# Weight sums moved into the first down stage, projection weights split without a rounded copy, and another place for small states, in a streaming encoder step

## The chip, the cores and the metric

One core of one Trainium2 chip runs the whole program. Its engines are TensorE (PE in the profile, PEld its weight loads), VectorE (DVE), ScalarE (ACT), GpSimd (POOL) and SyncE (SP), which here issues nearly all DMAs from one queue. The metric is the device time of one execution in microseconds, and the median of the runs counts. All numbers are float32; products are made from high and low parts of float32 operands.

## The reference, cut to what matters

The reference is one layer over 1024 prompt tokens and 64 sample tokens of width 1024:

```
h = x + 0.5 * (silu(n(x) @ Wg) * (n(x) @ Wu)) @ Wd      # first FFN, inner width 2816
z = n(h) @ w_in            -> u | q | k | v
y_ssm = GLU(S5(u)); y_att = DiffAttn(q, k, v)
h = h + concat(y_ssm, y_att) @ w_out
h = h + CrossAttn(n(h), n(mem))
x = h + 0.5 * (second FFN)(n(h));  final RMSNorm
```

The outputs are the normed tokens, the new keys and values, the last S5 states and the memory's keys and values. `w_out` and the rows of `Wd` are inputs, so everything that depends on them alone can be computed at any time before it is used.

## The kernel before, in words

**The products.** Activations lie feature by token, 128 features by 1088 tokens (a "row" of the pool `rows`, which has 36 of them). Each float32 product is three matmuls, from high and low parts of weight and operand (`mm3`, line 176 in the profile). Large products are made in Winograd's form: seven products of half-sized blocks in place of eight, with sums of weight quarters and sums of activation quarters. The sums of gate/up weights are made on POOL beside the products (`mixed`, lines 672 to 675). The sums of down weights are made on POOL by `down_sums` (lines 502 to 510) and stored in DRAM (`down_d`), those of the square products (`w_out`, `w_cq`, `w_co`) by `weight_sums` (lines 442 to 450, `sums_d`); both load weight quarters on SP, do four additions on POOL (lines 506 to 509 and 446 to 449) and store.

**The split.** A weight tile of 128x512 is split by `split_into` (lines 152 to 154): ACT writes the rounded high part `hi` to SBUF and a second rounded copy `q` to the one buffer of a PSUM pool `pr`; DVE subtracts `q` from the raw tile. With `staged=False` `w_split` (lines 162 and 163) leaves the copy out, and DVE subtracts `hi`, which lies in SBUF. `units` (line 183), which makes the 16 input projections and the 4 GLU products, uses the staged form; the memory projections use the other.

**The first FFN.** `ffn` first makes gate and up for 22 blocks j of the inner width. After the first five blocks `aside(j)` takes one step of the generator `side` after each product, seven in a block. The side of the first FFN is a chain: `s5_params` (S5 coefficients, small DVE operations, then transposes on PE in line 1086), `diff_lambda`, `s5_prep` for four groups, and `down_sums` for all blocks of the down product, with the four rows `prep` as its places and two steps for a piece. Of what is left when the blocks are done, `for _ in side: pass` issues the rest. Then the down product runs in three blocks b (`DOWN`: 4, 8 and 8 rows of Wd), each in seven factors q of four products i. Each product is emptied by `residual` (line 783, DVE) or, for four factors of the first block, by ACT; `prepare` makes the next factor's weight split (lines 152 to 154) and operand (`value`, line 412; `operand`, lines 418 and 419), and `fetch` loads the weights of the third next factor. In the last block `join` (line 834) adds accumulators on POOL and DVE. Two last rows of Wd are done per output row: `residual`, then `mix_row`, which splits the row (lines 212 and 213), adds its square to the statistics (`Stats.add`, lines 259 and 260, POOL) and stores it.

**The stage after it.** `wide_powers` makes S5 powers on POOL in `wide_row`. Then come 16 input projections (`in_unit`); after each half of one, every generator in `bg` is taken a step: `weight_sums(0)` of `w_out` from the first unit on, four `s5_main` (the scans on DVE, products in lines 1344 and 1345, gelu on ACT in line 1346), and from the third head on `weight_sums` of `w_co` and `w_cq`. `s5_main` keeps small states `gs` (128x152, lines 1307 to 1325) in a buffer of the tag `ws`, of which there are four and in which `weight_sums` also has its quarters.

**What sets the order.** Of each engine and queue the instructions run in order. The order is planned when the program is built: instructions are taken by their place in the code as soon as a simulated timeline has their inputs and buffers free. A wait that lasts longer on the chip than in the plan holds all that is behind it on its engine.

## Time and profile before

| | us |
|---|---|
| median of 3 runs | 2386.49 |
| lowest and highest | 2383.15, 2392.55 |
| the profiled execution | 2393.03 |
| its span, first to last instruction | 2391.2 |
| mean granted TensorE clock | 0.980 |

In the profile PE is TensorE, DVE VectorE, ACT ScalarE, POOL GpSimd, SPq SP's DMA queue. L176 is line 176 of the kernel. `r<-b,r` is a tile written and the tiles read (b is a PSUM bank, r a row, wr, ws, wh and wl weight tiles). A clock of 1.00 is 2.4 GHz, 0.50 is 1.2 GHz. "Idle before it" is the time for which the engine had nothing to run, with what ended it.

### The profile page before, as it was taken

Reading aid. Unit: us, or ns where it says so; the run is one execution under the profiler, and the core shown is the slowest. Engines: PE = TensorE matmul, PEld = TensorE weight load, DVE = VectorE, ACT = ScalarE, POOL = GpSimd, SP = SyncE. Lnnn points to the kernel's source line nnn. Section 1 sums busy time; section 2 is a strip of 40 time slices with the busy share of each in tenths; the row PEclk is TensorE's granted clock in tenths of the full one; section 3 lists DMA queues with packets and bytes.
Section 4 is the critical chain, followed back from the end, with each engine's and each line's share of the span. In section 5 each row is a group of like instructions: output and inputs, shape, how many; then the busy total and the mean of one; then the engine's idle time right before and its main releaser. Section 6 shows DMA issues by size and latency. Waiting matters only on the chain.

```text
span 2391.2 us, 45853 instructions
## 1 busy us (share of the span) xinstructions
PE 2265.2 (95%) x16914; PEld 2202.8 (92%) x16914; DVE 1599.6 (67%) x3318; ACT 1289.3 (54%) x2506; POOL 1083.4 (45%) x1048
## 2 busy tenths in 40 slices
PE   6999999998999898998999999898999999999998
PEld 6999999998999897997789999798899999999998
DVE  7666344336888688238988788788655555568897
ACT  6554445446554421237866766676544545466543
POOL 1567777882018704425510500024788886630050
PEclk9999999998999998999999999999999999999999
DMA  6232444678434647864336541152255452265422
GB/s 214 80 109 76 121 127 132 221 248 312 141 125 147 202 127 206 257 187 146 116 118 198 180 154 41 49 188 91 87 163 174 161 165 87 76 224 172 164 69 85
DMA packets 374316, 354.97 MB, mean 148 GB/s; under 512 B 42654, under 2 KB 313035, under 8 KB 374091
## 3 DMA queue, kind: packets, MB, share of 16 engines
q1 hardware_dynamic: 374000, 352.01, 46.5%
q8 instruction: 133, 2.18, 0.4%
q14 instruction: 93, 0.75, 0.1%
q10 hardware_dynamic: 90, 0.02, 0.0%
HBM read 245.23 MB, written 102.14 MB: 145 GB/s over the span
## 4 chain that ended last, share of the span: by engine, by line
PE 57%; DVE 14%; POOL 11%; DMA 8%; issue 4%; ACT 3%; SPq 1%; DVEq 0%; POOLq 0%; ACTq 0%
PE b L176 49%; PE b L138 2%; DMA r<-w_ffn_d 2%; PE b L1761 2%; DMA down_d<-r 2%; DMA wr<-w_ffn_gu 2%; DVE wl L154 2%; POOL r L715 1%; DVE r L419 1%; POOL wr L674 1%; PE b L1508 1%; POOL ws L675 1%; POOL ws L673 1%; POOL ws L672 1%; POOL r L702 1%
## 5 line engine op out<-in xcount | busy, mean ns | idle before, releaser
L176 PE MATMUL b<-r,wh 128*128 128x272 f32 (+4 forms) x9600 | 1690.8, 296 | 54.8 <-DVE r L783 15.1
L176 PEld LDWEIGHTS b<-r,wh 128*128 128x128 f32 x9600 | 1422.8, 191 | 71.1 <-DVE r L783 17.4
L176 PE MATMUL b<-r,wl 128*128 128x272 f32 (+4 forms) x4800 | 1058.3, 295 | 8.1 <-DVE wl L154 8.1
L176 PEld LDWEIGHTS b<-r,wl 128*128 128x128 f32 x4800 | 787.9, 191 | 10.2 <-DVE wl L154 9.9
L652 DVE TENSOR_TENSOR r<-b,r 128x272 f32<-128x272 f32 x440 | 172.0, 434 | 253.5 <-PE b L176 152.1
L153 ACT CAST q<-wr 128x512 fp32r<-128x512 f32 x280 | 166.2, 594 | 240.6 <-DVE wl L154 232.1
L154 DVE TENSOR_TENSOR wl<-wr,q 128x512 fp32r<-128x512 f32 x280 | 190.8, 681 | 147.9 <-issue 82.8
L152 ACT CAST wh<-wr 128x512 fp32r<-128x512 f32 x280 | 172.7, 621 | 193.3 <-PE b L176 189.0
L154 DVE TENSOR_TENSOR wl<-ws,q 128x512 fp32r<-128x512 f32 x206 | 140.5, 682 | 108.6 <-ACT q L153 70.0
L834 POOL TENSOR_TENSOR r<-r,r 128x544 f32<-128x544 f32 x40 | 64.6, 1621 | 321.0 <-DVE r L783 311.6
L419 DVE TENSOR_TENSOR r<-r,r 128x544 fp32r<-128x544 f32 x224 | 175.0, 799 | 36.9 <-ACT r L418 36.3
L153 ACT CAST q<-ws 128x512 fp32r<-128x512 f32 x206 | 121.8, 591 | 140.6 <-DVE wl L154 94.9
L152 ACT CAST wh<-ws 128x512 fp32r<-128x512 f32 x206 | 127.5, 621 | 123.1 <-PE b L176 96.8
L593 POOL TENSOR_TENSOR r<-r,r 128x544 f32<-128x544 f32 x28 | 43.6, 1559 | 280.1 <-ACT r L592 279.4
L418 ACT CAST r<-r 128x544 fp32r<-128x544 f32 x224 | 144.5, 649 | 22.9 <-DMA r<-hid_d 22.6
L783 DVE SCALAR_TENSOR_TENSOR r<-b,r 128x272 f32<-128x272 f32 (+4 forms) x328 | 133.3, 441 | 34.8 <-PE b L176 28.9
L672 POOL TENSOR_TENSOR ws<-wr,wr 128x512 f32<-128x512 f32 x44 | 61.4, 1395 | 138.3 <-DMA wr<-w_ffn_gu 128.1
L138 PE MATMUL b<-ident,r 128*128 128x128 f32 (+4 forms) x649 | 94.7, 283 | 24.0 <-DMA r<-g_subln 9.9
L715 POOL TENSOR_TENSOR r<-r,r 128x1088 f32<-128x1088 f32 x44 | 112.0, 2545 | 9.4 <-ACT r L714 9.4
L138 PEld LDWEIGHTS b<-ident,r 128*128 128x128 f32 (+4 forms) x649 | 76.2, 145 | 36.1 <-DMA r<-x_prompt 9.9
L446 POOL TENSOR_TENSOR ws<-ws 128x128 f32<-128x128 f32 x48 | 32.5, 678 | 150.6 <-DVE r L1269 63.7
L153 ACT CAST q<-r 128x512 fp32r<-128x512 f32 x90 | 53.0, 588 | 86.8 <-DVE wl L154 86.8
(348 smaller groups left out, 2950.2 us busy)
## 6 DMA issues: line engine op xcount, KB each, us to landing
wr<-w_ffn_gu SPq DMA_DIRECT2D x194, 256.0 KB, 3.0
r<-w_ffn_d SPq DMA_DIRECT2D x100, 256.0 KB, 4.4
hid_d<-r SPq DMA_DIRECT2D x44, 544.0 KB, 2.8
r<-hid_d SPq DMA_DIRECT2D x44, 544.0 KB, 6.2
down_d<-r SPq DMA_DIRECT2D x40, 512.0 KB, 4.0
h_d<-r SPq DMA_DIRECT2D x48, 272.0 KB, 2.4
r<-h_d SPq DMA_DIRECT2D x48, 272.0 KB, 4.0
sums_d<-ws SPq DMA_DIRECT2D x48, 256.0 KB, 3.1
```

The lines of the kernel that those rows point to most:

```text
L138: T.transpose(out, in_, ident[:n, :n])
L152: A.copy(hi, x)
L153: A.copy(r, x)
L154: V.tensor_tensor(out=lo, in0=x, in1=r.bitcast(F32), op=ALU.subtract)
L176: T.matmul(pc[:, :c1 - c0], w, x[:, c0:c1], start=(first + i == 0 and q == 0), stop=(first + i == n - 1 and q == 2))
L418: A.copy(r[:, 0], v)
L419: V.tensor_tensor(out=r[:, 1], in0=v, in1=r[:, 0].bitcast(F32), op=ALU.subtract)
L652: V.tensor_tensor(out=oc, in0=pc, in1=tc_, op=ALU.add)
L672: G.tensor_tensor(out=s1, in0=r[2], in1=r[3], op=ALU.add)
L715: G.tensor_tensor(out=up, in0=up, in1=gate, op=ALU.mult)
L783: V.scalar_tensor_tensor(out=hc_, in0=pc, scalar=0.5, in1=hc_, op0=ALU.mult, op1=ALU.add)
L834: (V if n_ else G).tensor_tensor(out=o_, in0=o_, in1=x_, op=ALU.add)
```

## The change

It makes the sums of the last block of the first down product, and all of `weight_sums(0)` for `w_out`, in a new generator `later`, which takes steps during the down products: after odd products of factors 1 to 6 in the first block, after each product in the other two. Both use the four rows `prep`; the 32 loads and 16 stores of `w_out`'s sums, and 16 loads and 8 stores of the last block's, move with them in SP's queue. `s5_params` takes seven steps more. `units` splits its weights without the rounded copy. `gs` moves from a `ws` buffer to columns of `wide_row`, which is made 1088 wide; columns 512 to 768 are also scratch of `wide_powers`.

```diff
@@ -180,7 +180,7 @@
 
 
         n = len(xs)
-        ws = [load_w(src) for src in wsrcs]
+        ws = [load_w(src, False) for src in wsrcs]
         ps_ = [[bank() for _ in range(3)] for _ in ws]
         for k0, k1 in ((0, at or n), (at or n, n)):
             for w, p in zip(ws, ps_):
@@ -431,17 +431,25 @@
 
     sums_d = dram([3, 4, 4, P, 4, P], "sums_d")
 
-    def weight_sums(n, w, swap=False):
+    def weight_sums(n, w, swap=False, places=None, pause=0):
+
 
         i11, i21, i12, i22 = (1, 0, 3, 2) if swap else (0, 1, 2, 3)
         for k in range(4):
-            ts = [half([P, 4, P]) for _ in range(4)]
+            if places:
+                ts = [z[:, c:c + 512].rearrange("p (i n) -> p i n", i=4) for z in places()[2 * (k % 2):2 * (k % 2) + 2]
+                      for c in (0, 512)]
+            else:
+                ts = [half([P, 4, P]) for _ in range(4)]
             for c, t in enumerate(ts):
+                yield from steps(pause)
                 for h in range(2):
                     wj = w[(4 * h + k) * P:(4 * h + k + 1) * P].rearrange("p (h c n) -> p h c n", h=2, c=4)
                     load(out=t[:, 2 * h:2 * h + 2], in_=wj[:, :, c])
-            yield
+            if not places:
+                yield
             for c, t in enumerate(ts):
+                yield from steps(pause)
                 a11, a21, a12, a22 = (t[:, i] for i in (i11, i21, i12, i22))
                 G.tensor_tensor(out=a22, in0=a21, in1=a22, op=ALU.add)
                 G.tensor_tensor(out=a21, in0=a11, in1=a21, op=ALU.subtract)
@@ -489,10 +497,11 @@
 
     down_d = [dram([10, 2, P, 4, 256], "down_d%d" % i) for i in range(2)]
 
-    def down_sums(dst, w, blocks, places, pause):
+    def down_sums(dst, w, blocks, places, pause, first=0):
+
 
         pairs = [(js[k], js[k + len(js) // 2]) for js in blocks for k in range(len(js) // 2)]
-        todo = [(n, c, w[j0 * P:(j0 + 1) * P], w[j1 * P:(j1 + 1) * P]) for n, (j0, j1) in enumerate(pairs) for c in range(2)]
+        todo = [(n, c, w[j0 * P:(j0 + 1) * P], w[j1 * P:(j1 + 1) * P]) for n, (j0, j1) in enumerate(pairs, first) for c in range(2)]
         places, prev = places(), None
         for i in range(len(todo) + 1):
             if i < len(todo):
@@ -625,7 +634,7 @@
                 V.tensor_copy(ssq[:n, t0:t1], p.rearrange("p (t n) -> p t n", n=P)[:n, 0:t1 - t0, 0])
             return rsqrt_mean(ssq, D, [P, 9], "rs")
 
-    def ffn(ops, w_gu, w_d, src_d, rb, between, side=iter(()), ordered=False, on_row=None, on_chunk=None):
+    def ffn(ops, w_gu, w_d, src_d, rb, between, side=iter(()), ordered=False, on_row=None, on_chunk=None, later=iter(())):
 
 
         wg = w_gu.rearrange("(k p) m -> p k m", p=P)
@@ -846,6 +855,8 @@
                     down_rest(q)
                 for i in range(4):
                     p = d.product(q, i)
+                    if b or q and i % 2:
+                        next(later, None)
                     for pc, oc_ in parts(p, acc[i][q]):
                         if b == 0 and q in (0, 2, 3, 4):
                             A.mul(oc_, pc, 0.5)
@@ -865,6 +876,8 @@
                 if last:
                     join(q)
 
+        for _ in later:
+            pass
         down_rest(7)
         items = [None] * KT
         for m in range(KT):
@@ -1036,11 +1049,11 @@
         dt = small([16, 2], "dt")
         ldt = small([16, 2], "ldt")
         load(out=ldt, in_=a["ssm_log_dt"][0].rearrange("(j q) -> j q", q=2))
-        yield from steps(2)
+        yield from steps(3)
         exp_small(ldt, dt)
         are, aim = tmp[:, 0], tmp[:, 1]
         x, th, n, r, s = (tmp[:, i] for i in range(2, 7))
-        yield from steps(2)
+        yield from steps(3)
         dtb = dt.unsqueeze(2).to_broadcast([16, 2, 64])
         V.tensor_tensor(out=x.rearrange("j (q p) -> j q p", q=2), in0=are.rearrange("j (q p) -> j q p", q=2),
                         in1=dtb, op=ALU.mult)
@@ -1064,7 +1077,7 @@
         V.tensor_tensor(out=nat[:, 0], in0=e, in1=th, op=ALU.mult)
         V.tensor_tensor(out=nat[:, 1], in0=e, in1=x, op=ALU.mult)
         V.tensor_scalar(out=nat[:, 2], in0=nat[:, 1], scalar1=-1.0, scalar2=None, op0=ALU.mult)
-        yield from steps(2)
+        yield from steps(3)
 
         V.tensor_tensor(out=x, in0=are, in1=are, op=ALU.mult)
         V.tensor_tensor(out=th, in0=aim, in1=aim, op=ALU.mult)
@@ -1080,7 +1093,7 @@
         V.tensor_tensor(out=x, in0=x, in1=th, op=ALU.subtract)
         V.tensor_tensor(out=nat[:, 4], in0=x, in1=n, op=ALU.mult)
         V.tensor_scalar(out=nat[:, 5], in0=nat[:, 4], scalar1=-1.0, scalar2=None, op0=ALU.mult)
-        yield from steps(2)
+        yield from steps(5)
         p = bank()
         for i in range(8):
             tr(p[:, i * 16:(i + 1) * 16], nat[:, i])
@@ -1102,7 +1115,7 @@
             for n in (1, 2, 4):
                 cmul([x[:, n:2 * n] for x in v], [x[:, 0:n] for x in v], [x[:, n - 1:n] for x in v])
 
-        yield from steps(2)
+        yield from steps(3)
         prep.extend(row([P, 1024]) for _ in range(4))
         pows = prep[0][:, 0:256].rearrange("p (q n j) -> p q n j", q=2, n=8)
         pw = const([P, 8, NPAIR], "apow_r")
@@ -1304,7 +1317,7 @@
             scan(x, k, tu, f, (apr, api, apn))
             yield
 
-        gs = half([P, 152]).rearrange("p (r n) -> p r n", n=19)
+        gs = wide_row[:, 512 + 152 * (f % 3):664 + 152 * (f % 3)].rearrange("p (r n) -> p r n", n=19)
         xe = x.rearrange("p r (s i) -> p r s i", i=8)[:, :, :, 7]
         V.memset(gs[:, :, 0:1], 0.0)
         V.tensor_copy(gs[:, :, 1:17], xe[:, :, 0:16])
@@ -1371,8 +1384,11 @@
         st1.add(h)
         store(out=h1_d[m], in_=h)
 
-    ffn(ops0, a["w_ffn1_gu"][0], a["w_ffn1_d"][0], h0_d, None, x_start(), chain(s5_params(), diff_lambda(), *(s5_prep(f) for f in range(4)),
-              down_sums(down_d[0], a["w_ffn1_d"][0], DOWN, lambda: prep, 2)), ORDERED, on_row=mix_row)
+    ffn(ops0, a["w_ffn1_gu"][0], a["w_ffn1_d"][0], h0_d, None, x_start(),
+        chain(s5_params(), diff_lambda(), *(s5_prep(f) for f in range(4)),
+              down_sums(down_d[0], a["w_ffn1_d"][0], DOWN[:2], lambda: prep, 2)),
+        ORDERED, on_row=mix_row, later=chain(
+            down_sums(down_d[0], a["w_ffn1_d"][0], DOWN[2:], lambda: prep, 3, 6), weight_sums(0, a["w_out"][0], False, lambda: prep, 1)))
     pump(1000)
 
 
@@ -1409,7 +1425,7 @@
         yield
 
 
-    wide_row = row([P, 768])
+    wide_row = row()
     wide = [wide_row[:, c:c + 128 * n].rearrange("p (i f j) -> p i f j" if n == 1 else "p (i f q j) -> p i f q j",
                                                  **(dict(i=8, f=4) if n == 1 else dict(i=8, f=4, q=2)))
             for c, n in ((0, 2), (256, 1), (384, 1))]
@@ -1431,7 +1447,6 @@
         G.tensor_scalar(out=wide[2], in0=wide[1], scalar1=-1.0, scalar2=None, op0=ALU.mult)
 
     wide_powers()
-    bg.append(weight_sums(0, a["w_out"][0]))
     for f in range(4):
         u = in_unit(f, True)
         pump_all()
```

## Rows read from the trace of the kernel before

**Rows 1.** The profile page, its first two parts: busy time of each engine with its share of the span and its instructions, and the TensorE clock that was granted, in tenths, over 40 equal slices of the span.

```profile
PE 2265.2 (95%) x16914; PEld 2202.8 (92%) x16914; DVE 1599.6 (67%) x3318; ACT 1289.3 (54%) x2506; POOL 1083.4 (45%) x1048
...
PEclk9999999998999998999999999999999999999999
```

**Rows 2.** Short stretches around the places where the granted clock fell. Columns: the stretch in us from the span's start, its length, busy us (and instructions) of PE, PE's weight loads, DVE, ACT and POOL, mean granted clock, busy share of the DMA engines, GB/s.

```profile
184.00:192.00 8.00, 6.84 (x34) 6.52 (x35) 7.23 (x21) 3.08 (x7) 0.78 (x1) 0.57 0.43 138
541.00:554.00 13.00, 8.95 (x38) 7.99 (x39) 8.67 (x12) 4.60 (x9) 9.49 (x10) 0.61 1.05 405
563.00:571.00 8.00, 7.03 (x34) 7.04 (x35) 6.41 (x14) 4.84 (x10) 0.00 (x0) 0.57 0.59 204
757.00:762.00 5.00, 4.84 (x26) 4.85 (x27) 3.20 (x8) 3.17 (x6) 5.00 (x7) 0.66 0.40 129
795.00:803.00 8.00, 5.37 (x20) 5.37 (x21) 8.00 (x15) 2.84 (x4) 7.92 (x9) 0.57 0.84 312
928.00:943.00 15.00, 9.44 (x35) 9.12 (x36) 14.79 (x43) 2.39 (x5) 9.50 (x12) 0.54 0.64 200
2327.00:2335.00 8.00, 6.40 (x29) 6.40 (x30) 6.65 (x13) 5.38 (x9) 3.11 (x2) 0.57 0.00 0
```

**Rows 3.** What TensorE (PE) waited for between 130 and 500 us, in the first FFN's gate/up products. Columns: waiter, what ended the wait, us in total, times, the longest.

```profile
PE b L138 <- DVE r L1065: 2.3, 1, 2.3
...
PE b L138 <- DVE r L1066: 1.2, 1, 1.2
PE b L138 <- DVE r L1064: 1.0, 1, 1.0
```

**Rows 4.** The same view for 500 to 575 us, where the gate/up products end and the down products begin.

```profile
PE b L176 <- ACT r L418: 5.2, 1, 5.2
PE b L176 <- DVE r L783: 3.2, 1, 3.2
PE b L176 <- DVE r L652: 1.1, 1, 1.1
PE b L176 <- DVE r L419: 1.1, 2, 0.7
```

**Rows 5.** The same view for 735 to 960 us: the end of the first down stage, its last rows, and the first two thirds of the input projections.

```profile
PE b L176 <- DVE r L783: 8.7, 3, 5.0
PE b L1344 <- ACT r L1346: 6.6, 1, 6.6
PE b L1344 <- ACT r L1403: 5.0, 1, 5.0
...
PE b L176 <- DVE r L213: 1.6, 1, 1.6
```

**Rows 6.** The chain that ended last, in order of time, one piece of it at the end of the gate/up products: start us, us, what.

```profile
536.91 8.97 DMA r<-hid_d
```

**Rows 7.** POOL's timeline at the same place: start us, us, line, operation, out<-in, count, and in brackets the idle time before it and what ended it.

```profile
548.71 1.25 POOL L506 TENSOR_TENSOR r<-r 128x256 f32<-128x256 f32 x1 [2.46 <-DMA r<-w_ffn_d]
```

**Rows 8.** Four longer stretches, columns as in rows 2: the boundary between gate/up and down products of the first FFN, the same boundary of the second FFN, the first down stage, and the S5 scans beside the input projections.

```profile
530.00:560.00 30.00, 23.61 (x156) 22.43 (x155) 12.91 (x20) 10.69 (x23) 16.36 (x16) 0.83 0.99 370
2110.00:2140.00 30.00, 29.64 (x234) 29.21 (x234) 21.34 (x34) 18.50 (x38) 11.09 (x5) 1.00 0.85 311
570.00:715.00 145.00, 145.00 (x1157) 144.99 (x1157) 119.09 (x221) 85.54 (x166) 6.26 (x4) 1.00 0.47 157
850.00:945.00 95.00, 86.07 (x565) 83.71 (x564) 92.62 (x235) 21.88 (x40) 27.36 (x32) 0.93 0.54 154
```

**Rows 9.** DVE's timeline between 776 and 826 us, the copies of the small S5 states (line 1312), columns as in rows 7.

```profile
794.79 0.41 DVE L1312 COPY ws<-cf 128x4 f32<-128x4 f32 x1 [7.63 <-DMA sums_d<-ws]
...
809.71 2.49 DVE L1312 COPY ws<-cf 128x4 f32<-128x4 f32 x1
```

**Rows 10.** ACT's timeline between 895 and 965 us, two neighbours in its queue, columns as in rows 7.

```profile
932.00 0.59 ACT L153 CAST q<-wr 128x512 fp32r<-128x512 f32 x1 [6.37 <-DVE wl L154]
932.52 0.39 ACT L1346 ACTIVATE r<-b 128x272 f32<-128x272 f32 x1
```

**Rows 11.** Groups of DVE instructions over the whole run, shapes apart: line, operation, names, shapes, count, busy us, mean ns of one, idle us before them and what ended it. First the low part of a split whose rounded copy q lies in PSUM (split_into), then the one that subtracts the high part in SBUF (w_split, not staged).

```profile
L154 DVE TENSOR_TENSOR wl<-wr,q 128x512 fp32r<-128x512 f32 x280 | 190.8, 681 | 147.9 <-issue 82.8 <-ACT q L153 46.6 <-PE b L176 14.0
...
L163 DVE TENSOR_TENSOR wl<-wr,wh 128x512 fp32r<-128x512 f32 x32 | 30.5, 967 | 19.2 <-ACT wh L162 18.9
```

**Rows 12.** The same view for POOL over the whole run: the additions of the weight sums, square (446, 447) and down (506).

```profile
L446 POOL TENSOR_TENSOR ws<-ws 128x128 f32<-128x128 f32 x48 | 32.5, 678 | 150.6 <-DVE r L1269 63.7 <-DMA ws<-w_co 52.4 <-DMA ws<-w_cq 19.4
L506 POOL TENSOR_TENSOR r<-r 128x256 f32<-128x256 f32 x40 | 30.6, 764 | 33.6 <-DMA r<-w_ffn_d 27.2 <-issue 5.4 <-DMA wr<-w_ffn_gu 0.9
...
L447 POOL TENSOR_TENSOR ws<-ws 128x128 f32<-128x128 f32 x48 | 26.9, 560 | 1.8
```

**Rows 13.** The same view for DVE between 570 and 715 us, the first down stage, in which POOL is nearly idle.

```profile
L419 DVE TENSOR_TENSOR r<-r,r 128x544 fp32r<-128x544 f32 x50 | 36.5, 744 | 5.5 <-ACT r L418 5.3
L783 DVE SCALAR_TENSOR_TENSOR r<-b,r 128x272 f32<-128x272 f32 x92 | 36.4, 435 | 9.0 <-PE b L176 8.8
L412 DVE TENSOR_TENSOR r<-r,r 128x544 f32<-128x544 f32 x24 | 18.2, 784 | 0.0
```

**Rows 14.** The same view for DVE between 725 and 765 us, the end of that stage, where POOL is busy almost throughout.

```profile
L419 DVE TENSOR_TENSOR r<-r,r 128x544 fp32r<-128x544 f32 x8 | 8.1, 1027 | 0.0
```

**Rows 15.** What the DMA queue of SP waited for between 570 and 715 us, its longest; columns as in rows 3.

```profile
SPq L476 <- DVE wl L154: 41.5, 20, 4.8
```

## The prediction

> **What bounds the kernel now.** I read the page first. TensorE is busy for 2265.2 us of 2391.2 and its clock is full in most slices [rows 1]. The change takes no matmul away, so it can only pay where TensorE stands still, or works at half clock after it stood still. That is some 126 us of idle time and a few slow stretches, and the question is which of them the edits touch. So next I went through the stretches of fallen clock and TensorE's waits around them. The clock has two levels, 1.00 and 0.50, and each fall follows a pause. In a stretch with mean clock c the share at half clock is (1-c)/0.5, and the loss is half of the busy time in it. From [rows 2]: 184 to 192 us costs 6.84 x 0.86 / 2 = 2.9 us; 541 to 554, 3.5; 563 to 571, 3.0; 757 to 762, 1.6; 795 to 803, 2.3; 928 to 943, 4.3.
>
> The waits in front of them are four places, each with an edit that bears on it. **S**, S5 coefficients: 2.3 + 1.2 + 1.0 us for DVE [rows 3], with the clock 7.4. **B**, the boundary from gate/up to down products: 5.2 + 3.2 + 1.1 + 1.1 [rows 4], with the clock (3.5 + 3.0) 17.1. **R**, the last rows of the down product: one wait of 5.0 among three for L783, and 1.6 for L213 [rows 5], with the clock 8.9. **P**, the projections beside the S5 scans: 6.6 us for a bank that ACT empties [rows 5], with the clock 10.9; another 5.0 us there ends with L1403. Together 44 us, or 49 with the last one: the ceiling.
>
> **Part by part.**
>
> **Seven steps more in s5_params.** The transposes of line 1086 reach TensorE before DVE's small operations are done. Four of the seven steps lie between those operations and the transposes. A step is one product of 24 matmuls; 1157 matmuls fill 145 us [rows 8], 0.125 us each, so a step is 3.0 us. Four are 12 us against 4.5 us of lateness. No work is added, and the later side work has room (next paragraph). I take 6 of 7.4.
>
> **A shorter side.** Steps are taken for blocks 5 to 21, seven each: 119. The side before needs 12 for the parameters, 1 for lambda, 4 x 17 for the preparation and 21 x 2 for the down sums: 123. Four steps, two pieces of down sums, are left when the blocks end, and are issued just there. The trace shows this: POOL makes its last down sums at 548.71, after a wait for their load [rows 7], while the first operand of the down product takes 8.97 us to arrive [rows 6] and the DMA engines are full (1.05, 405 GB/s) [rows 2]. After, it is 19 + 1 + 68 + 13 x 2 = 114, so the side ends five steps early, and its loads, stores and additions are out of the way. The nearest row for that is the second FFN, whose side (21 x 5 = 105 of 126 steps) ends early already: there the boundary has 29.64 us of TensorE in 30, against 23.61 here [rows 8]. One difference: the four rows `prep` now stay taken. The down stage then needs 14 rows of sums, 8 of inputs, 8 operands, 2 of weights and these 4, 36 of 36; the two rows for the last rows of Wd come after the sums are done. It fits, with nothing spare. Bounds: 0 (the loads are as slow anyway) to 17.1. I take 13, nearer to the second FFN's row.
>
> **Small states.** At 787 us DVE stood for 7.63 us before a copy of 128x4 into a `ws` buffer, which a store of `w_out`'s sums still held [rows 9]. The emptying of the tail's banks (L783) is behind it in DVE's queue, and TensorE's wait of 5.0 us for L783 is that. After, neither the sums nor the buffer are there. The copy is instead bound to `wide_powers`, whose scratch covers columns 512 to 768, so it can move behind the last rows, where the powers end on POOL; DVE is then between two projections. POOL also loses its 64 additions there, which held DVE: a copy of 128x4 took 2.49 us [rows 9]. But the additions of row squares stay. I take 7 of 8.9, bounds 0 and 8.9.
>
> **Split without the copy.** 36 copies (32 for the projections, 4 for GLU) leave ACT. Their 0.59 us each hide under TensorE; what counts is their order. ACT's copy waits 6.37 us until DVE has read the one buffer q, and the gelu that would empty a bank for TensorE is next in its queue [rows 10]; that is P. After, ACT waits for raw weights and free tiles alone. Against a full gain: DVE is busy for 92.62 us of 95 there [rows 8], so TensorE may only run ahead until it needs a low part or an emptied bank. And DVE's own instruction changes: with q in PSUM it takes 681 ns, with `hi` in SBUF 967 [rows 11]. For the 17 or so of these in the scans that is at most 17 x 0.29 = 4.9 us. I take 8 of 10.9, bounds 3 and 15.9 (with the L1403 wait).
>
> **The moved sums.** For the last down block 32 additions, for `w_out` 64 go to POOL in the down stage: 32 x 0.76 + 16 x 0.68 + 48 x 0.56 = 62 us [rows 12], where POOL has 6.26 us of work in 145 [rows 8]. The deadlines are met in the code: the down sums end after 27 of 68 steps, in the second block's factor 3, and are first fetched in its factor 6; `w_out`'s end at step 60, in the last block's factor 4. SP's queue gets 72 DMAs more. It already stands for L154 to free raw tiles (41.5 us in 20 waits) [rows 15], that is, it runs ahead of need; weights are fetched two to three factors, 24 us or more, ahead. I price this at nothing; without that cover TensorE would stand for as long as a fetch is late.
>
> DVE is the doubtful one. A factor of a full block gives it 4 x (0.784 + 0.744) for operands [rows 13], 4 x 0.68 for weights [rows 11] and 8 x 0.435 for emptying, 12.3 us, against 4 x 3.0 = 12 us of TensorE; three of seven factors have no L412 and leave room. Over the stretch it has 145 - 119 = 26 us free [rows 8]. With POOL busy, L419 takes 1027 ns in place of 744 [rows 13, 14]. Below: 0, if POOL's additions fall on instructions that read PSUM. Above: all 82 of L419 and L412 slowed by 0.28, 23 us, still within 26 in sum, but late locally by up to 8 x 0.28 = 2.3 us in each of four factors in a row, 9 us a block. I take 5 us, because POOL will be busy for about a third of the time, not throughout.
>
> The Trainium skill ("SBUF — State Buffer", "Who interferes with whom") says that VectorE with two SBUF inputs and GpSimd reading SBUF exclude each other for a whole instruction, and that VectorE with one SBUF input does not meet this. The trace agrees on the kinds (681 against 967 ns). By its full block, the sum for this part would be up to 62 us of DVE in place of my 23, and the split would be a loss wherever POOL works.
>
> At the end of the last block nothing is gained: its other waits for L783 (3.7 us) have a like in the second FFN, where no square sums run and the clock's loss is 6.40 x 0.86 / 2 = 2.8 us against 1.6 here [rows 2].
>
> **Sum.** -6 - 13 - 7 - 8 + 5 = -29 us. The profiled execution took 2393.03 us (span 2391.2), which gives 2364.0; it lies 6.5 above the median of the three runs, 2386.49, so against that the forecast is 2357.5.
>
> **Rivals.**
>
> *All waits go* (0.16): the L1403 wait too, and the moved sums cost nothing: 2386.5 - 49.3 = 2337. For it: the second FFN's clean boundary. Against: DVE's load in the scans.
>
> *The waits move* (0.19): DVE stays the bound in the scans (gain 2), the small states wait for `wide_powers` behind the squares on POOL (gain 2), the boundary is bound by loading 8 inputs and weights whatever the side does (gain 6), S gives 4, the moved sums cost 6: -8, 2378. The order of every queue is planned anew from a timeline that does not hold these blocks, so a new wait of a few us can stand anywhere.
>
> *POOL holds DVE* (0.11), the one that ends slower. Place: the second and third down block. Mechanism: each of the 96 additions keeps a DVE instruction of operand preparation waiting for its whole length. Price: 62 us less 26 of room = 36, and with some six pauses of TensorE, each with 2 to 3 us at half clock as in [rows 2], 15 more: 2386.5 - 34 + 51 = 2403. It begins to cost at 26 us of holding and decides against the change at about 26 + 34 - 15 = 45. For it: the L419 row; against: that row shows 0.28 us a piece, not 0.6. The page named above states this mechanism.
>
> **How the numbers follow.** The forecast's own case has 0.54, at 2345 to 2370. About 0.5%, 12 us, is what a measurement of this kernel can tell from no change. Faster by more: 0.54 + 0.16 = 0.70; within: 0.19; slower: 0.11. The range goes from the first rival to beyond the second, with the cost of the moved sums at its local bound: 2336 to 2390; outside it is the third and little else.
>
> **What would show it.** S: no wait for L1064 to L1066. B: no L506 after the last gate/up product, the first operand in 4 to 6 us, TensorE over 28 us of 30. R: no L1312 wait on DVE, the row additions back to back. P: no L153 in the projections, no wait of L1344 for L1346; L163 near 0.7 to 0.97 us. Moved sums: 96 more additions inside the down stage, L419 at 0.8 to 0.9 us, TensorE's idle time there under 5 us. I am wrong if TensorE waits for L783, L419 or L154 in that stage for over 15 us, if DVE stands before a small state again, or if the boundary keeps its pause.

## The result, and the profile of the changed kernel

The changed kernel takes 2376.11 us (median of five runs, 2374.32 to 2379.24), 10.4 less than the 2386.49 of the kernel before. Its ratio to the kernel before is 0.9942, 95% interval [0.9927, 0.9958]: some 14 us, between 10 and 17, so that the two medians lie near the lower end; 29 were forecast. The profiled execution took 2374.69 us (span 2372.7). Its span is 18.5 us shorter than that of before, but the execution profiled before lay 6.5 above its median and this one 1.4 below. From here on a run is compared by its ratio to the kernel before, timed on the same chip beside it.

The page, for [rows 1]:

```profile
PE 2251.8 (95%) x16914; PEld 2191.2 (92%) x16914; DVE 1599.9 (67%) x3318; ACT 1268.9 (53%) x2470; POOL 1090.5 (46%) x1048
```

ScalarE lost its 36 copies; TensorE is busy for 13.4 us less with the same matmuls, for the most part because fewer of them run at half clock (its mean granted clock is 0.984, before 0.980). Now the waits of TensorE: first the gate/up products (130 to 490 us, for [rows 3]), then the boundary to the down products (490 to 570, [rows 4]), then the tail, the last rows and the projections (735 to 960, [rows 5]). Columns as there.

```profile
PE b L176 <- DVE r L661: 3.4, 3, 1.6
PE b L1230 <- DMA r<-r: 0.3, 1, 0.3
```
```profile
PE b L176 <- DVE r L792: 2.6, 1, 2.6
PE b L176 <- DVE r L419: 2.5, 2, 1.9
PE b L176 <- DVE r L661: 0.8, 1, 0.8
PE b L176 <- ACT r L418: 0.5, 1, 0.5
```
```profile
PE b L269 <- POOL r L260: 14.7, 1, 14.7
PE b L176 <- DVE r L792: 3.5, 1, 3.5
PE b L176 <- DVE r L1422: 2.5, 1, 2.5
PE b L138 <- DVE rsy L232: 2.3, 1, 2.3
...
PE b L176 <- ACT r L1359: 1.2, 2, 0.6
```

The three waits of S are gone. The boundary has 6.4 us of idle time in place of 10.6. Of the 8.7 us for the emptying of the tail's banks (L783, now L792) 3.5 are left, and the 6.6 and 5.0 us of the projections are gone. But one wait has grown: 14.7 us for L260, the addition of row squares on POOL, which L269 needs to make the norm of the first projection. In the kernel before it was:

```profile
PE b L269 <- POOL r L260: 1.1, 1, 1.1
```

POOL's timeline there in the changed kernel (columns as in [rows 7]):

```profile
780.32 1.52 POOL L457 TENSOR_TENSOR ws<-ws 128x128 f32<-128x128 f32 x1
781.80 2.54 POOL L260 TENSOR_TENSOR r<-r,r 128x1088 f32<-128x1088 f32 x1
784.29 1.52 POOL L456 TENSOR_TENSOR ws<-ws 128x128 f32<-128x128 f32 x1
...
791.90 3.58 POOL L260 TENSOR_TENSOR r<-r,r 128x1088 f32<-128x1088 f32 x1
...
800.43 0.45 POOL L455 TENSOR_TENSOR ws<-ws 128x128 f32<-128x128 f32 x1
...
808.78 2.47 POOL L260 TENSOR_TENSOR r<-r,r 128x1088 f32<-128x1088 f32 x1
```

Between the seven row-square additions stand additions of weight sums (L454 to L457). They are those of `w_co` and `w_cq`, which in the code come with the third head of the projections, and in the kernel before ran beside the projections. The seven take 29.5 us from the first start to the last end, of which they are busy for 19.0. The rows themselves came quicker: ScalarE made the seven squares that L260 adds within 17.6 us (their ends lie at 771.5 to 789.1 us), where the kernel before took 33.3 (783.2 to 816.5). But POOL, which had sums of `w_co` ahead of them, began the first L260 10.3 us after its square, and ended the last 22.1 us after the last square.

The stretches, for [rows 8] (columns as there): the boundary in the kernel before and in the changed one, 45 us each from 7 us before the first operand (first L418), then the down stage and the scans in the changed one.

```profile
536.00:581.00 45.00, 35.44 (x226) 34.03 (x225) 25.09 (x41) 26.04 (x57) 12.76 (x11) 0.81 0.85 314
```
```profile
522.00:567.00 45.00, 38.62 (x267) 37.43 (x266) 28.03 (x43) 26.09 (x57) 26.55 (x28) 0.89 1.02 370
556.00:701.00 145.00, 143.84 (x1146) 143.62 (x1146) 123.93 (x219) 84.24 (x165) 57.94 (x82) 1.00 0.69 237
842.00:937.00 95.00, 89.12 (x595) 86.49 (x594) 88.49 (x238) 16.97 (x32) 14.93 (x21) 0.98 0.63 174
```

At the boundary 41 more matmuls fit into 45 us, 41 x 0.125 = 5.1 us. In the down stage POOL now works for 58 us, and TensorE is busy for 143.84 of 145, where before it was busy throughout: it loses 1.2. In the scans POOL has 15 us of work where it had 27, and the clock is 0.98 where it was 0.93.

The table gives where the time lies, read from TensorE's timeline: from the start to the first S5 matmul (first L1308), from there through the scans to their last matmul (last L1358), from there to the attention (first L1523), and the rest, which ends with TensorE's last matmul, some 10 us before the span does. The experiments stand beside, under the names that they have below; every time is of one profiled execution, in us.

| kernel | to first S5 matmul | scans | to attention | rest | ratio to before, 95% |
|---|---|---|---|---|---|
| before | 843.7 | 150.0 | 91.3 | 1295.8 | 1 |
| changed | 840.0 | 140.1 | 91.3 | 1291.1 | 0.9942 [0.9927, 0.9958] |
| s5_only | 835.8 | 151.7 | 91.3 | 1294.3 | 0.9973 [0.9959, 0.9987] |
| staged_back | 833.3 | 152.0 | 92.9 | 1295.0 | 0.9962 [0.9948, 0.9976] |
| both_back | 830.0 | 147.3 | 104.5 | 1301.5 | 1.0021 [1.0007, 1.0035] |
| wout_back | 839.4 | 160.4 | 91.3 | 1292.1 | 1.0023 [1.0010, 1.0036] |
| gs_half | 829.7 | 147.0 | 102.0 | 1296.7 | 0.9986 [0.9975, 0.9996] |
| staged | 839.2 | 143.0 | 91.3 | 1293.9 | 0.9950 [0.9934, 0.9966] |
| split_only | 845.1 | 147.6 | 104.4 | 1294.8 | 1.0057 [1.0041, 1.0073] |
| split_edge | 846.7 | 148.0 | 93.8 | 1298.0 | 1.0027 [1.0016, 1.0038] |
| hold | 829.8 | 164.6 | 91.3 | 1291.4 | 1.0011 [0.9997, 1.0025] |
| hold_cq | 844.5 | 143.8 | 91.3 | 1288.5 | 0.9942 [0.9927, 0.9957] |
| hold_mid | 831.1 | 145.9 | 91.3 | 1292.0 | 0.9925 [0.9908, 0.9943] |
| down_two | 841.6 | 139.2 | 91.3 | 1294.0 | 0.9941 [0.9928, 0.9955] |
| down_hold | 838.5 | 139.9 | 91.3 | 1294.3 | 0.9918 [0.9902, 0.9933] |
| down_two_hold | 832.4 | 142.0 | 91.3 | 1297.5 | 0.9909 [0.9892, 0.9926] |
| co_down | 839.0 | 136.3 | 91.3 | 1290.8 | 0.9909 [0.9891, 0.9926] |
| co_hold | 838.0 | 137.3 | 92.8 | 1292.8 | 0.9907 [0.9891, 0.9923] |
| co_down_hold | 834.5 | 136.9 | 91.3 | 1293.5 | 0.9896 [0.9877, 0.9916] |
| co_two_hold | 845.8 | 137.1 | 91.3 | 1291.8 | 0.9903 [0.9889, 0.9918] |

The rest differs by up to 13 us (1288.5 to 1301.5), and why stays open; 4.7 of the 18 us between the first two rows lie there. The columns are therefore only a guide to where time went, and the ratio decides.

### The profile page after: what moved, and what is told of

Its sections match the earlier page's. It is cut to its first block, busy times and chain, and to the rows that moved or that the text cites. A ratio compares the mean times of both kernels' runs of the same rounds, so it can differ in the third digit from the quotient of the medians.

```text
span 2372.7 us, 45778 instructions
## 1 busy us (share of the span) xinstructions
PE 2251.8 (95%) x16914; PEld 2191.2 (92%) x16914; DVE 1599.9 (67%) x3318; ACT 1268.9 (53%) x2470; POOL 1090.5 (46%) x1048
## 4 chain that ended last, share of the span: by engine, by line
PE 61%; DVE 13%; POOL 9%; DMA 7%; issue 5%; ACT 2%; SPq 1%; DVEq 0%; POOLq 0%; ACTq 0%
PE b L176 52%; PE b L138 2%; PE b L1776 2%; DMA wr<-w_ffn_gu 1%; DVE wl L154 1%; DVE r L419 1%; PE b L1523 1%; PE b L1559 1%; DMA down_d<-r 1%; POOL r L724 1%; POOL wr L683 1%; POOL r L711 1%; DVE r L792 1%; POOL r L843 1%; DMA r<-w_ffn_d 1%
## 5 line engine op out<-in xcount | busy, mean ns | idle before, releaser
L153 ACT CAST q<-wr 128x512 fp32r<-128x512 f32 x244 | 144.9, 594 | 174.9 <-DVE wl L154 167.5
L154 DVE TENSOR_TENSOR wl<-wr,q 128x512 fp32r<-128x512 f32 x244 | 166.2, 681 | 104.5 <-issue 50.1
L152 ACT CAST wh<-wr 128x512 fp32r<-128x512 f32 x244 | 150.5, 621 | 99.8 <-PE b L176 95.4
L419 DVE TENSOR_TENSOR r<-r,r 128x544 fp32r<-128x544 f32 x224 | 179.1, 818 | 29.8 <-ACT r L418 28.9
L153 ACT CAST q<-ws 128x512 fp32r<-128x512 f32 x206 | 121.7, 591 | 143.5 <-DVE wl L154 103.9
L792 DVE SCALAR_TENSOR_TENSOR r<-b,r 128x272 f32<-128x272 f32 (+4 forms) x328 | 132.4, 438 | 31.7 <-PE b L176 25.5
L418 ACT CAST r<-r 128x544 fp32r<-128x544 f32 x224 | 144.3, 649 | 16.7 <-DMA r<-hid_d 16.3
L162 ACT CAST wh<-wr 128x512 fp32r<-128x512 f32 x68 | 41.5, 619 | 182.4 <-PE b L176 141.5
L1504 POOL CAST r<-r 64x256 fp32r<-64x256 f32 x32 | 12.8, 399 | 193.6 <-PE b L138 181.7
```

What stands on the lines that cost most here:

```text
L152: A.copy(hi, x)
L153: A.copy(r, x)
L154: V.tensor_tensor(out=lo, in0=x, in1=r.bitcast(F32), op=ALU.subtract)
L418: A.copy(r[:, 0], v)
L419: V.tensor_tensor(out=r[:, 1], in0=v, in1=r[:, 0].bitcast(F32), op=ALU.subtract)
L792: V.scalar_tensor_tensor(out=hc_, in0=pc, scalar=0.5, in1=hc_, op0=ALU.mult, op1=ALU.add)
```

## Experiments

Line numbers in what was expected are those of the changed kernel or of the kernel before, whichever the text names; an edit can shift them by one to four.

**1. Is the new stall the missing gain?** In the run *hold* all four additions of each of `w_co`'s and `w_cq`'s sums are queued behind the last row-square addition.

```diff
-                G.tensor_tensor(out=a22, in0=a21, in1=a22, op=ALU.add)
+                with tc.issue_after(st1.last.ins) if n else nullcontext():
+                    G.tensor_tensor(out=a22, in0=a21, in1=a22, op=ALU.add)
...
```

> The changed kernel with one edge of order more: GpSimd's additions for the sums of w_co and w_cq (64 of each) are queued behind the last row-square addition (L260). Theory 1, the missing gain is the new stall at 796.58 us (14.72 of idle, 2.29 behind it, and 23.89 us of half clock after it), made by those additions standing between the L260s: the seven L260 follow one another, the stall is at most 2 us, the half clock there goes, and the time falls from 2376.1 by 15 to 20 us to 2356-2361. Rival A, the L260s are late because VectorE (L213 and the row additions) holds GpSimd off the SBUF, with or without the sums: a stall of over 8 us stays, and the time is 2370-2377. Rival B, the sums of w_co and w_cq are then late for their products: the stall goes and another of like size stands before the cross-attention or in the projections, 2370-2378.

1.0011 [0.9997, 1.0025]: the whole gain lost. The stall went as theory 1 said (first S5 matmul at 829.8 in place of 840.0), but the scans grew from 140.1 to 164.6 us: rival B, and more than its size. TensorE's longest waits from 850 to 1000 us, and the longest of SP's queue from 830 to 990:

```profile
PE b L1358 <- ACT r L1360: 13.4, 2, 12.9
PE b L1358 <- DMA r<-m_d: 6.4, 1, 6.4
PE b L1309 <- DMA r<-u_d: 6.2, 2, 3.2
```
```profile
SPq L459 <- POOL ws L458: 17.0, 12, 5.1
...
SPq L448 <- DMA sums_d<-ws: 8.2, 6, 3.5
```

`u_d` holds the inputs of the scans and `m_d` a matrix for their products, and their loads stand in SP's queue behind loads and stores of the sums (L448, L459) that wait for POOL and for a free buffer. The chain of work that ended last in this stretch goes the same way, from a sum on POOL through that queue to a load for the scan (start us, us, what):

```profile
870.95 0.92 POOL ws L458
...
873.55 3.79 DMA r<-u_d
```

So the early sums are what makes the stall and what frees the scans.

**2. Which part let the sums run early?** *gs_half* undoes the first of these edits, *wout_back* the second, *both_back* both.

```diff
-        gs = wide_row[:, 512 + 152 * (f % 3):664 + 152 * (f % 3)].rearrange("p (r n) -> p r n", n=19)
+        gs = half([P, 152]).rearrange("p (r n) -> p r n", n=19)
...
-            down_sums(..., DOWN[2:], lambda: prep, 3, 6), weight_sums(0, a["w_out"][0], False, lambda: prep, 1)))
+            down_sums(..., DOWN[2:], lambda: prep, 3, 6)))
...
     wide_powers()
+    bg.append(weight_sums(0, a["w_out"][0]))
```

> The changed kernel with the small states (gs) back in one of the four half buffers that the weight sums use. Theory 1, with an addition: in the kernel before, a sum of w_co could not take its buffers before the small states had let go of theirs, so these buffers were a brake on the sums; the change took the brake away. With it back, no L454-L457 stands before the seventh L260, the stall at 796.58 goes; and since the sums of w_out are no longer in these stages, the small states wait for nobody either (no wait over 1 us of VectorE at their first write): 2356-2362, as with the edge of order. Rival C, the room for small states was worth the predicted 7 us and is needed beside the moved w_out sums: the 7.63 us wait of VectorE comes back and 5 us of TensorE with it, 2363-2370 if the stall goes, 2383 if it does not. Rival A (contention, not order): stall stays, 2376-2383.

> The changed kernel with the sums of w_out back in the projections and only the last down group's sums in the first down stage. Theory 1: GpSimd's additions (now those of w_out, then w_co, w_cq) still stand between the L260s, since what holds a sum back is its buffers and the small states have left these: a stall of 10 to 16 us before the first projection stays, and the time is 2374-2382. If the moved w_out sums alone had opened the slot (rival D), the stall goes and the time falls to 2358-2364.

> The changed kernel with two parts undone together: the sums of w_out back in the projections and the small states back in the half buffers. What is left is the steps of s5_params, the last down group in the first down stage and the split without a copy. Theory 2: start to the first L419 keeps its 14 us against before; the wait of the small states (5 us of TensorE) and the stalls of the projections are as before, so the two parts undone are worth nothing net: ratio 0.992 to 0.996, the same as the changed kernel. Rival G, the two parts together brought what the prediction gave them (7 us, and more in the projections): ratio 0.997 to 1.001.

*gs_half*: the stall is gone, the seven L260 run with no sum between them, and the time is 0.9986, not the 2356 to 2362 us expected. The first addition for `w_co` starts at 876 us, in the changed kernel at 712. TensorE's waits from 780 to 1050 us show what came instead:

```profile
PE b L176 <- ACT r L1419: 7.7, 1, 7.7
PE b L1357 <- DMA r<-m_d: 7.3, 2, 6.6
...
PE b L1358 <- DMA r<-rk_d: 2.6, 1, 2.6
...
PE b L269 <- POOL r L260: 1.1, 1, 1.1
```

So the small states in the `half` buffers were a brake: a sum of `w_co` gets its four buffers only after they are done. *wout_back* has the stall (15.0 us) without the moved `w_out`: it is the freed buffers, not the freed time on POOL, that let sums in, as theory 1 said. Its time missed: 1.0023, where 2374 to 2382 us, less than before, were expected. Its scans take 160.4 us, with sums in them again. The four versions make a square, all with the other parts of the change in: nothing 1.0021, room for the states alone 1.0023, `w_out` moved alone 0.9986, both 0.9942. *both_back* missed its expectation (0.992 to 0.996); it is nearest to rival G (0.997 to 1.001). The two parts bring 19 us together, far more than predicted, and without them the kernel is no faster than before although S and B are in it; so something else in the change must cost.

**3. How many early?** *hold_cq* queues only `w_cq`'s 64 additions behind the row squares (`if n == 1`), *hold_mid* also the last 16 of `w_co`'s (`or n and k == 3`).

> The changed kernel with the edge of order for the sums of w_cq alone: their 64 additions are queued behind the last row-square addition, those of w_co stay where the planner put them. The run that held both took the stall before the first projection away (down stage to first S5 matmul 13 us shorter) and lost 24 us in the projections, where the loads and stores of 128 late additions stood between the transfers of the S5 scan in SP's queue. Theory 2: both costs have one source, the same 128 additions, and what matters is how many are left for the projections. With half of them early the stall is at most 6 us, the projections (first S5 matmul to the first of the attention, 231 us in the changed kernel, 261 with all held) take 231 to 238, and the time is 0.988 to 0.992 of the kernel before, 2364-2373 on this chip. Rival F, any addition in the projections costs as much as it does in the stall: 245 us or more there, ratio 0.995 to 1.000.

> As the run before, and the last quarter of w_co's sums (16 additions) held too, 80 in all, so that no addition stands between the row-square additions. Theory 2: the stall goes altogether (at most 2 us), the projections take 234 to 242 us, ratio 0.988 to 0.993. Rival F: ratio 0.996 to 1.001.

0.9942 and 0.9925. *hold_cq* missed: L260 was still waited for (4.5 us, then 3.7 for L232), and its first FFN took 6.5 us more (first L418 at 535.8 us, 529.3 in the changed kernel), for which I have no cause. *hold_mid* has no such wait and scans of 145.9 us, between 140.1 and 164.6: theory 2's trade by number of additions, at a gain of 4 us over the changed kernel that the intervals don't tell from zero.

**4. The split without a copy.** *staged* puts the copy back into the changed kernel, *staged_back* into *both_back*, *split_only* is the kernel before with the change's edit alone (the diff backwards).

```diff
-        ws = [load_w(src, False) for src in wsrcs]
+        ws = [load_w(src) for src in wsrcs]
```

> The changed kernel with the projection weights split by way of the rounded copy again (ScalarE's L153 back, VectorE's subtraction from it). By the prediction's step the copy is worth 8 us: the L153 holds the gelu again, a stall of 5 to 7 us near 930 us comes back with half clock behind it, 2381-2386. Rival E, the stall that went at 930 went for another reason (the other order of the work before it) and the split costs VectorE what it saves ScalarE: 2373-2378. The stall at 796 stays in either case.

> The run with w_out's sums and the small states undone (1.0021 of before, 0.0048 above the one with the s5_params steps alone), and now the split by way of the rounded copy as well: what is left is the steps of s5_params and the last down group's sums in the first down stage. In that run TensorE stood 8.66 us at 1029 us for L1419 on ScalarE, which stood behind an L153 whose load of w_out's sums was late by SP's queue. Theory 3, the split without a copy lets ScalarE run ahead to that L153 sooner and so costs there what it saves: without it no stall over 3 us at 1029, ratio 0.994 to 0.997. Rival J, the moved down group orders the later work anew and the split is innocent: the stall stays, ratio 1.000 to 1.003.

> The kernel before with the split of the projection weights without the rounded copy, alone. The prediction's step gave it 8 us (3 to 15.9): ratio 0.9935 to 0.9985 with the stalls of TensorE behind L1346 and L1403 gone. Theory 3 (those stalls go only when the sums leave the projections, and ScalarE's freed time is spent waiting at a later L153): ratio 0.999 to 1.005, and a stall of 5 to 10 us for L1403 after 1020 us.

Alone, the split makes the kernel slower: 1.0057, some 14 us, more than even theory 3 allowed (0.999 to 1.005). With the sums still in the projections, it is 1.0021 with it and 0.9962 without. In the changed kernel it is 0.9942 with it and 0.9950 without, which the intervals don't tell apart; there the stalls at 930 us stay away even with the copy (one of 3.5 us is left). So the 19 us of experiment 2 hold only with the new split: with the copy, making room for the states and moving `w_out` take the kernel from 0.9962 to 0.9950, which is not told from zero. These numbers fit that the two mostly kept the sums away from where the split costs; that is argued, not shown by itself. ScalarE's timeline in *split_only* at the place of the loss, TensorE's wait there, and the same place in the kernel before:

```profile
1051.52 0.59 ACT L153 CAST q<-ws 128x512 fp32r<-128x512 f32 x1 [19.51 <-DMA ws<-w_out]
1052.04 0.61 ACT L162 CAST wh<-wr 128x512 fp32r<-128x512 f32 x1
1052.56 1.06 ACT L1403 COPY r<-b 128x512 f32<-128x512 f32 x2
```
```profile
PE b L176 <- ACT r L1403: 8.5, 2, 8.3
```
```profile
1038.15 0.59 ACT L1403 COPY r<-b 128x512 f32<-128x512 f32 x1 [0.31 <-PE b L138]
1045.75 0.59 ACT L153 CAST q<-ws 128x512 fp32r<-128x512 f32 x1 [7.02 <-DVE r L203]
1046.28 0.58 ACT L1403 COPY r<-b 128x512 f32<-128x512 f32 x1
```

With its order planned anew, ScalarE has the first weights of the output product (an L153 from `ws`) ahead of a pair of L1403, which empties two banks for TensorE. The load for it stands in SP's queue behind loads and stores for the sums of `w_cq`, and ScalarE stands for 19.5 us until it comes. To test that, *split_edge* queues those weights' copies behind the last L1403 (`tok[0]`):

```diff
...
-                self.w[q, k] = self.held.split_w(self.raw[q, k])
+                with tc.issue_after(tok[0]) if tok[0] is not None else nullcontext():
+                    self.w[q, k] = self.held.split_w(self.raw[q, k])
...
```

> The kernel before with the split without the rounded copy alone (1.0057 of before, with 8.32 us of TensorE's idle time at 1044.88 for L1403, behind an L153 of w_out's sums that waited 19.51 us), and one edge of order more on ScalarE: the copies and splits of the output product's weights are queued behind the last L1403. Nothing else changes. Theory 3, the loss is that L153's place in ScalarE's order: no stall over 3 us for L1403 and no half clock there, the stage from the last L1345 to the attention goes back from 104.42 to 91-93 us, ratio 0.9985 to 1.001. Rival K, the L153 is only where the wait shows and the projections are bound by the late sums, which then hold up the output product itself: a stall of like size for w_out's sums or L1403 remains within the next 100 us, ratio 1.004 to 1.007.

The stall and its half clock went, the stage from 104.4 to 93.8 us, as expected, but the ratio is 1.0027 [1.0016, 1.0038], above the expected 1.001. So that order is about half of the 14 us (the two ratios differ by 7). Another 3 us show before the first projection: *split_only*, *split_edge* and *both_back* take 26.5 us from the first L269 to the first S5 matmul, some 7 of them at half clock, where the kernel before takes 23.5, all at full clock. The rest stays open.

**5. The steps of s5_params alone.** *s5_only* is the kernel before with the longer pauses:

```diff
-        yield from steps(2)
+        yield from steps(3)
...
-        yield from steps(2)
+        yield from steps(5)
```

> The kernel before with the longer pauses of s5_params alone. By the prediction's step 6 us (ceiling 7.4) are gained: the three waits of TensorE for L1051 to L1053 go, and everything after runs as before: ratio 0.9965 to 0.998, 2384-2388 on this chip. Rival H, the later end of the side work moves the down sums' loads into the boundary and gives it back: ratio 0.999 to 1.001.

0.9973 [0.9959, 0.9987], 6.5 us, and the three waits gone: as predicted.

**6. The boundary.** *down_two* moves a second down group into the down stage:

```diff
-              down_sums(down_d[0], a["w_ffn1_d"][0], DOWN[:2], lambda: prep, 2)),
+              down_sums(down_d[0], a["w_ffn1_d"][0], DOWN[:1], lambda: prep, 2)),
...
-            down_sums(down_d[0], a["w_ffn1_d"][0], DOWN[2:], lambda: prep, 3, 6), ...
+            down_sums(down_d[0], a["w_ffn1_d"][0], DOWN[1:], lambda: prep, 1, 2), ...
```

> The changed kernel with the second down group's sums moved into the first down stage too (pause 1), so that the side work beside the gate/up products ends earlier still. The prediction gave the shorter side 13 us at the boundary from gate/up to down; the runs with one group moved show 30.6 us of TensorE's work in the 37 us from 528 on, 28.2 with the s5_params steps alone. Theory 4, what is left there is the boundary's own transfers (share of the DMA engines 1.02, wr<-down_d 8.76 us and r<-h_d 6.27 us in the chain), which a still shorter side does not relieve: 29.5 to 32 us in a window of 37 us from the same place, and the second block of the down stage waits for its sums, ratio 0.994 to 1.000. Rival L, the side's last sums still are the bound: 34 us or more, ratio 0.988 to 0.992.

0.9941, and the same x267 at the boundary as the changed kernel. I took that for theory 4, until POOL's timeline showed when the sums run. Its additions in the changed kernel from 400 us to the boundary at 529 (columns as in [rows 12]):

```profile
L515 POOL TENSOR_TENSOR r<-r 128x256 f32<-128x256 f32 x16 | 11.9, 742 | 17.3 <-DMA r<-w_ffn_d 15.3 <-DVE wl L154 1.4 <-ACT wh L152 0.6
L516 POOL TENSOR_TENSOR r<-r 128x256 f32<-128x256 f32 x16 | 11.8, 740 | 0.1
L518 POOL TENSOR_TENSOR r<-r 128x256 f32<-128x256 f32 x15 | 11.1, 743 | 0.1
L517 POOL TENSOR_TENSOR r<-r 128x256 f32<-128x256 f32 x15 | 11.1, 741 | 0.2
```

62 of the first FFN's 80, though only 48 stand beside gate/up in the code; in *down_two* 62 too, of 16; in the kernel before 76, in *s5_only* 64. So the place in the code did not set how many ran before the boundary; that the planner issues a sum as soon as its tile is free would explain it, and the next two runs take that freedom away. The other 18 of the changed kernel followed within 37 us of the first L418, in the first block of the down stage. So *down_two* had not tested the boundary. *down_hold* and *down_two_hold* queue the moved groups' loads on SP behind the down stage's own fetches (`mk[0]` is the last of them issued so far):

```diff
-                for h in range(2):
-                    load(out=t[:, 2 * h:2 * h + 2], ...)
+                with tc.issue_after(mk[0]) if first else nullcontext():
+                    for h in range(2):
+                        load(out=t[:, 2 * h:2 * h + 2], ...)
```

> In every version run so far 62 to 64 of the 80 additions for the first FFN's down sums, and their loads, run before the boundary from gate/up to down, whatever group stands in the down stage in the code: the planner pulls them forward. Here the changed kernel has its last group's loads queued on SP behind the down stage's own fetches, so that 48 additions run before the boundary and 32 after. If the prediction's step B had the right mechanism (the last sums' transfers are in the way of the first operands), TensorE does at least 290 matmuls in the 45 us from 7 us before the first L419 (226 in the kernel before, 267 in the changed one) and 4 to 8 us are gained: ratio 0.991 to 0.9925. Rival M, the boundary's own loads set it: 260 to 275 matmuls, ratio 0.993 to 0.996.

> The same with the last two groups in the down stage and queued there: 16 additions before the boundary, 64 after. By step B's mechanism 300 matmuls or more in those 45 us, and a wait at the second block if its sums come late: ratio 0.989 to 0.994. Rival M: at most 280 there, and the wait at the second block makes it 0.996 to 1.001.

Now 48 and 16 additions run before the first operand. The boundary, in *s5_only*, *staged_back*, *down_hold* and *down_two_hold*, 45 us each:

```profile
526.00:571.00 45.00, 36.19 (x233) 35.11 (x233) 24.70 (x38) 23.43 (x51) 25.71 (x28) 0.81 1.01 373
```
```profile
525.00:570.00 45.00, 37.84 (x255) 36.56 (x254) 28.44 (x42) 25.52 (x55) 25.93 (x28) 0.85 1.00 362
```
```profile
522.00:567.00 45.00, 41.43 (x308) 41.22 (x307) 30.14 (x48) 29.02 (x64) 20.33 (x19) 0.92 0.95 338
```
```profile
514.00:559.00 45.00, 44.45 (x354) 44.24 (x354) 33.03 (x52) 31.33 (x70) 24.80 (x23) 1.00 0.95 339
```

226, 233, 255, 267, 308, 354 matmuls: with two groups past it the boundary has no pause left, 16 us (128 x 0.125) better than before, and the times are 0.9918 and 0.9909, as expected. Only the second is clear of the changed kernel's interval, and barely. Theory 4 and rival M fall: the transfers and additions of the sums were the cost, as the prediction's step B had it. The runs do not tell the transfers from the additions.

**7. Versions that the causes point to.** *co_down* makes `w_co`'s sums in the down stage too, *co_hold* also holds the last 16 of `w_cq`'s, *co_down_hold* is *co_down* with the last down group held as above, *co_two_hold* with two.

```diff
-            down_sums(..., DOWN[2:], lambda: prep, 3, 6), weight_sums(0, a["w_out"][0], False, lambda: prep, 1)))
+            down_sums(..., DOWN[2:], lambda: prep, 2, 6), weight_sums(0, a["w_out"][0], False, lambda: prep, 1),
+            weight_sums(2, a["w_co"][0], False, lambda: prep, 1)))
-            bg.append(chain(weight_sums(2, a["w_co"][0]), weight_sums(1, a["w_cq"][0], True)))
+            bg.append(weight_sums(1, a["w_cq"][0], True))
```

> The changed kernel carried one step further: the sums of w_co are made in the first down stage too, behind those of w_out in the same four tiles (the pause between the last down group's sums is 2 in place of 3, to make room), so that 64 additions are left for the stretch before the projections in place of 128. Theory 2 (the additions cost where they stand between the row squares or in the projections, and little in the down stage): the stall before the first projection falls from 14.7 us to at most 7, the projections stay at 231 us or below, the down stage grows by at most 2 us; ratio 0.987 to 0.991. Rival I, GpSimd's additions hold VectorE in the down stage (64 more of them, up to 0.4 us each on its path) or their loads delay the stage's own: the down stage grows by 8 us or more, ratio 0.994 to 0.998.

> As the run before, with the last quarter of w_cq's additions (16) queued behind the last row-square addition, so that none stands between those. Theory 2: the stall falls to 2 us or less, the projections take 231 to 236 us, ratio 0.985 to 0.990. Rival I: 0.993 or more.

> The version with w_co's sums in the down stage (0.9909 of before), with the last down group's loads queued behind the down stage's fetches. By step B's mechanism 4 to 8 us below that: 0.987 to 0.9895. Rival M: 0.990 to 0.993; and if the down stage now has too much to load (its DMA engines were busy for 0.88 of the time), a growth of that stage by 3 us or more, 0.992 to 0.995.

> What the runs point to, put together: the sums of the last two down groups, of w_out and of w_co in the first down stage, the down groups' loads queued on SP behind the stage's own fetches; the sums of w_cq stay before the projections. If the gains add (boundary as with two groups held: 353 matmuls in 45 us, no half clock; stall before the first projection at most 6 us; projections at most 229 us from the first S5 matmul to the attention): ratio 0.985 to 0.989. If the down stage is now full (it has 145 us, and the additions there rise to 64 + 64 + 64): it grows by 4 us or more, or the sums of w_co slip out of it to before the projections again: 0.989 to 0.993.

0.9909 [0.9891, 0.9926], 0.9907 [0.9891, 0.9923], 0.9896 [0.9877, 0.9916] and 0.9903 [0.9889, 0.9918]. *co_down* beats both kernels: the wait for L260 falls to 4.8 us, POOL has nothing to do in the scans, and these take 136.3 us. In *co_hold* that wait is gone, but the ratio, expected at 0.985 to 0.990, is no better. The best is *co_down_hold*, some 25 us under the kernel before and just outside the 0.987 to 0.9895 expected; its lead over *co_down* is within the intervals. In *co_two_hold* the gains don't add. The boundary is clean, but TensorE then stands 10.7 us for L794 at 749 us and 9.0 for L260: sums meant for the down stage run over into the tail.

## Why the prediction was wrong

Three steps of the prediction failed: in B that the side would be out of the way, in R that POOL would have less to do, and in P that the split would pay. The cost of the moved sums was too high by 4 us.

**S** was right: 6 us predicted, 6.5 measured alone.

**B**, 13 us: the mechanism was right, and *down_two_hold* shows even more than its size. What failed is the step "the side ends five steps early, and its loads, stores and additions are out of the way". I counted steps of the code, but moved sums were pulled forward, 62 additions ran before the boundary where the code has 48, and the other 18 within 37 us behind it. What was left came to 5.1 us by the count of matmuls. The last group's place in the code alone is worth 0.9973 to 0.9962, not told from zero.

**R**, 7 us: VectorE's wait at the small states did go, and the rows came quicker, as predicted. VectorE's timeline of these copies, for [rows 9]:

```profile
793.03 2.48 DVE L1325 COPY r<-cf 128x4 f32<-128x4 f32 x1
...
823.88 0.41 DVE L1325 COPY r<-cf 128x4 f32<-128x4 f32 x1 [1.75 <-POOL r L1446]
```

What failed is "POOL also loses its 64 additions there": it lost those of `w_out` and got 105 of the 128 of `w_co` and `w_cq`, which start before the first S5 matmul. The room given to the states was also room for the next sums, and these pushed the row squares back: from the first square to the norm's first matmul it is 39.8 us, where it was 37.0, and in *hold*, without these sums, 32.4. In exchange the scans were freed of those sums, 9.9 us. The rival *the waits move* had both in words, "the order of every queue is planned anew" and "a new wait of a few us can stand anywhere", and its 2378 is nearest to the result. I gave it 0.19, because I had no place for the wait. That its sum fits is in part luck: it has 6 us of cost for the moved sums, where 1.2 show, and no price for a new wait. The place could have been found: the buffers that hold back each sum, and what comes next for them.

**P**, 8 us of the sum: the wrong sign. Alone the step costs 14 us; in the changed kernel it brings nothing that can be measured. What failed is "what counts is their order" followed by a look at one copy only. The L153 that held the gelu did go, and 6.3 us for `m_d` and 2.5 for `rk_d` (in *split_only*) stood right behind it; and another L153, that of the next stage, moved ahead of the copies that empty banks. The waits of [rows 5] in the projections went in the changed kernel because POOL's sums left the scans, not because of the split: with the copy back (*staged*) the scans take 143.0 us, not the 150.0 of before, and with the copy back and the sums in the scans (*staged_back*) 152.0, with waits of 6.3 and 6.6.

**Moved sums**, 5 us of cost: the mechanism was right, the size too large. VectorE's instructions in the down stage of the changed kernel, for [rows 13]:

```profile
L419 DVE TENSOR_TENSOR r<-r,r 128x544 fp32r<-128x544 f32 x50 | 40.4, 828 | 3.5 <-ACT r L418 3.2 <-DMA wr<-down_d 0.3
...
L412 DVE TENSOR_TENSOR r<-r,r 128x544 f32<-128x544 f32 x24 | 19.6, 834 | 0.0
```

Against 744 and 784 ns that is 50 x 0.084 + 24 x 0.050 = 5.4 us of VectorE, inside its 26 us of room, and 1.2 us of TensorE's idle time. The Trainium skill's rule ("SBUF — State Buffer", "Who interferes with whom") holds here for the kinds of instruction: those with two SBUF inputs rose, and L792, which reads a bank and one row, did not (430 ns, before 435). The 62 us of VectorE that I had by it did not come (5.4 us did), and part of the waiting fell on POOL: of the 64 additions for `w_out`, the 31 that began while L419 or L412 ran took 0.89 us on average, the 21 that met none of these 0.46. The end of the last block stayed as predicted (3.5 us).

With what was measured, S 6.5, B 4.2 (5.1 less the 7 matmuls that S alone brings there) and 1.2 of cost for the moved sums come to 9.5 us, near the 9 of *staged_back*, which has neither the room for the small states nor `w_out`'s new place nor the split. These three, 15 us in the forecast, add some 5 us to it, which the intervals do not tell from nothing: 0.9962 [0.9948, 0.9976] without the three, 0.9942 [0.9927, 0.9958] with them.

## What to carry to other kernels

Where a planner orders the queues, a step's place in the code says what it gives way to, not when it runs: ask for each moved piece which buffer or queue holds it back now, and what takes the place that it leaves. A buffer that two kinds of work share can be the brake that keeps one of them out of the other's way, so that taking the sharing away removes one wait and lets another in. And an instruction taken from an in-order engine is worth its wait only if the next one in the queue is ready; look two waits deep.

## What the runs showed that was not expected

POOL pays for VectorE's work, and not only the other way round. An addition of 128x128 took 0.45 us while VectorE stood idle (at 800 us, above) and 1.52 while it ran L213, an instruction of two SBUF inputs that itself took 1.34 us at 770 us and 3.14 at 787 us, where a row-square addition had started ahead of it. A row-square addition took 2.47 us in the stretch where VectorE stood idle and up to 3.58 before.

A pause at the boundary costs more than its idle time: in the 48 us from 8 us before the first L418, TensorE of the kernel before stands for 9.6 us and is granted half clock for some 17; in *down_two_hold* it stands for 0.6 us and has full clock throughout.
